# Put-off second steps, ACT's own sum for v's mean, a product on GpSimd and re-ordered early loads in a two-layer hybrid decoder kernel

## The chip, the cores and the metric

The kernel runs on one core of a Trainium2 chip. The metric is the device time of a run in microseconds (us), the median of three runs. TensorE is written PE (its weight loads PEld), VectorE DVE, ScalarE ACT, GpSimd POOL, and SyncE, which issues nearly all loads, SP. All weights come from HBM in each run (163 MB), all arithmetic is in 32 bits.

## What is computed

Two layers (DEPTH) on 256 tokens of 1,024 features, then a last normalization:

```python
def hybrid_layer(x, ...):
    h = rmsnorm(x, norm_mix)
    cb, cc, cu, q, k, v, g, ga, gb = split(h @ w_in)         # 1024 -> 9216
    y_conv = (cb * conv3(cc * cu)) @ w_conv_out               # causal, 3 taps per channel
    y_ret = retention(rotary(q), rotary(k), v), per head: (o - mean(o)) * rsqrt(var(o)), * silu(g), @ w_ret_out
    merged = sigmoid(ga) * y_conv + sigmoid(gb) * y_ret
    x = x + merged @ w_o
    h2 = rmsnorm(x, norm_mlp)
    return x + square(relu(h2 @ w_up)) @ w_down               # 1024 -> 4096 -> 1024
```

The kernel takes the mean of o over a head's features out of v instead: v minus its own mean over the head (the function `value`).

## The kernel before, in words

**Blocks.** The weights are cut into 152 blocks of 1 MB, in the order of use; activations lie with features on partitions and the 256 tokens along the free dimension. Each block is one step of the program, a *window* (`window`, `proj`). A layer has 76: v (4 blocks), then `IN_ORDER`: g, g, (cc, cu, cb) twice, q, q, k, k, (cc, cu, cb) twice, g, g, ga x4, gb x4; then the products with w_conv_out (4), w_ret_out (4), w_o (4), w_up (16) and w_down (4 x 4 blocks into one sum).

**Two parts of every operand.** An fp32 value is written as a rounded fp32r part (hi) and the rest (lo): `split` makes hi with a copy on ACT (L103) and lo with a subtraction on DVE (L104). A block's product is 16 matmuls of 512 columns (hi weight by both parts of the activation) and 16 of 256 (lo weight by the activation's hi), all on PE at L165. So every block of weights costs two ACT casts and two DVE subtractions of 128x1024 (`split_block`, two halves), in tiles of the program's names `raw` (2 buffers) and `parts` (3 buffers). Block i+2 is split in window i; the load of block i+3 is issued at that window's end, on SP.

**Order.** Nothing schedules this: the engines run their instructions in the order in which the code emits them. `at(n, fn, ...)` puts a step in the list of the window n further on; in one window the list's steps of phase 0 come first, in the order in which they were put in, then the first half of block i+2, the steps of phase 1, the second half, and then the block's matmuls. What the list emits for one engine therefore stands ahead of that engine's share of the splitting of block i+2.

**Evictions.** The product of block i is in one of three PSUM buffers (`ps_main`); in window i+1 it is taken out by `collect`: an ACT copy of one half (L235) and a DVE sum of both (L236) to SBUF. What follows it is the function named after the operand: `gate`, `conv_u`, `conv_in`, `conv_b`, `conv_out`, `rotate`, `merge_gate`, `up_out`, `add_to_x`. `up_out` goes on in the same window with a ReLU (L710) and a square (L711) on ACT; the product with the norm's factor is on POOL one window later (L712) and the split of u another window later. `value` is v's: DVE sums 4 x 256 columns (L462), scales the sum (L463), and ACT and DVE make hi (L467), lo (L468) and v1 (L472) out of PSUM in turns. `conv_out` multiplies by cb on DVE (L518) and splits in the same window. `weigh_scores` weighs on DVE (L534, L535) and splits at once. `head_roots` to `head_out` make 1/std of a head: square root on ACT (L572), reciprocal on DVE (L577) one window later, a Newton step the next, the product (L587) and its split in the two windows after. `add_to_x` adds to x (L683) and splits the sum for the next norm (L271 on ACT, L276 on DVE) at once, then squares it between the two halves of the block's split.

**The tail of each sum.** `head_sums` makes PE sum the squares of a head (tile `var_ps`) behind a window's block; it needs the split of `osq` of that window. `norm_total` does the same for a norm.

Of the kernel before, what the change touches and what calls it, by code (L numbers as in the profile page):

```python
# [11 lines left out]
F32 = mybir.dt.float32  # L12
# [3 lines left out]
AF = mybir.ActivationFunctionType  # L16
# [36 lines left out]
def trunk_kernel(ctx, tc, px, pos, w, cst, mask, out):  # L53
# [260 lines left out]
    k0 = 0  # L314
    for n in (1, 3, 4):
        c = slice(n_par + k0 * T if k0 else 0, n_par + (k0 + n) * T)
        nc.scalar.dma_start(out=px_sb[:, c], in_=px[:, c])
        k0 += n
    for c in (slice(0, 4), slice(4, 8), slice(8, 16)):
        nc.sync.dma_start(out=raws[0][:, c, :], in_=w0[:, c, :])  # L320
    nc.sync.dma_start(out=raws[1].rearrange("p a b -> p (a b)"), in_=w[1])

# [75 lines left out]
    for layer in range(DEPTH):  # L398
# [59 lines left out]
        def value(i, ps):  # L458

            mu = small.tile([P, 2, 2], F32, tag="mu", name="mu")  # L460
            vs = ps.rearrange("p j (h f) -> p j h f", f=T)
            nc.vector.tensor_reduce(out=mu, in_=vs, axis=mybir.AxisListType.X, op=ALU.add)  # L462
            nc.vector.tensor_scalar(out=mu, in0=mu, scalar1=-1.0 / T, scalar2=None, op0=ALU.mult)  # L463
            for n in range(2):
                h = 2 * i + n
                hi, lo = v0_parts[:, 0, h, :], v0_parts[:, 1, h, :]
                nc.scalar.activation(hi, vs[:, 0, n, :], AF.Identity, bias=mu[:, 0, n:n + 1])  # L467
                nc.vector.scalar_tensor_tensor(  # L468
                    out=lo, in0=vs[:, 0, n, :], scalar=mu[:, 0, n:n + 1], in1=hi.bitcast(F32),
                    op0=ALU.add, op1=ALU.subtract,  # L470
                )
                nc.scalar.activation(v1[:, h, :], vs[:, 1, n, :], AF.Identity, bias=mu[:, 1, n:n + 1])  # L472
# [40 lines left out]
        def conv_b(p, ps_b):  # L513
            y = collect(ps_b)
            at(1, conv_out, p, y)

        def conv_out(p, y):
            nc.vector.tensor_tensor(out=y, in0=y, in1=conv[p], op=ALU.mult)  # L518
            split(y, *yc.pair(p))
# [12 lines left out]
        def weigh_scores(h, ps):  # L532
            t = t2("sc0")[:, 0, :]
            nc.vector.tensor_tensor(out=t, in0=ps[:, :T], in1=mask_sb[:, h, :], op=ALU.mult)  # L534
            nc.vector.tensor_tensor(out=sc1[:, h, :], in0=ps[:, T:], in1=mask_sb[:, h, :P], op=ALU.mult)  # L535
            split(t, sc0_parts[:, 0, h, :], sc0_parts[:, 1, h, :])
# [29 lines left out]
        def head_roots(i, st):  # L566
# [12 lines left out]
            for n in range(2):  # L579
                at(3 + n, head_out, 2 * i + n, rs[:, n, :])  # L580

        def head_out(h, rs):

            if h % 2 == 0:
                yr.tiles.append(s8.tile([P, KT // 2, 2, T], F32R, tag="s8", name=f"yr{h // 2}"))
            y = sg[:, 2 * h:2 * h + 2, :]
            nc.vector.tensor_tensor(out=y, in0=y, in1=both(rs), op=ALU.mult)  # L587
            split(y, *yr.pair(h))
# [89 lines left out]
        def add_to_x(p, ps, scale, norm, parts=True):  # L678

            for j in range(2):  # L680
                xk = x[:, 2 * p + j, :]
                for half in (1, 0):
                    nc.vector.scalar_tensor_tensor(  # L683
                        out=xk, in0=ps[:, j, half, :], scalar=scale, in1=xk, op0=ALU.mult, op1=ALU.add
                    )
            if parts:
                for j in range(2):
                    norm.split_hi(2 * p + j)
                for j in range(2):
                    norm.split_lo(2 * p + j)  # L690
            at(0, norm.square, p, ph=1)
            if p == NPAIR - 1:
                at(0, norm.fold, ph=1)
                at(1, norm.split_sum)

# [184 lines left out]
```

## Time and profile before

| | before |
|---|---|
| three runs, us | 946.89, 949.07, 946.75 |
| median, us | 946.89 |
| the profiled execution, us | 945.4 |
| its span, first to last instruction, us | 943.6 |
| PE / PEld busy in it, us (share) | 898.1 (95%) / 772.1 (82%) |
| DVE busy | 709.9 (75%) |
| ACT busy | 510.5 (54%) |
| POOL busy | 230.0 (24%) |
| chain that ended last, by engine | DVE 44%, PE 25%, ACT 18%, issue 8%, POOL 3%, DMA 3% |
| mean TensorE clock granted | 0.984 of full |

A matmul's end is modelled in the profile, so "busy" of PE is an upper bound of its useful time; the chain of work that ended last goes through DVE more than through PE. A row of a timeline reads: start in the span, time, engine, line, operation, output<-inputs, shapes, count; in brackets the engine's idle time before it and what ended it.

### The profile page before, as it was taken

The numbers are of one execution on the slowest core, as the hardware profiler recorded it, in microseconds if no ns is written. First come the engines' busy times: TensorE is split into PE (matmuls) and PEld (weight loads), VectorE is DVE, ScalarE is ACT, GpSimd is POOL, SyncE is SP. The second block draws the span as 40 slices with busy tenths as digits, with TensorE's granted clock in tenths as the row PEclk, the third lists the DMA queues.
The fourth block names the chain that finished last, engine by engine and source line by source line (L and its number), as shares of the span: only waits on it lengthen the run. The fifth ranks groups of instructions, "written<-read, shape, count | busy, mean of one in ns | idle before, by whom it ended". The sixth has DMA issues, their size and how long they took to land.

```text
span 943.6 us, 12548 instructions
## 1 busy us (share of the span) xinstructions
PE 898.1 (95%) x5026; PEld 772.1 (82%) x5026; DVE 709.9 (75%) x800; ACT 510.5 (54%) x709; POOL 230.0 (24%) x160
## 2 busy tenths in 40 slices
PE   9898999989999999999998999998999999999996
PEld 5687788877887887788887888887878887778896
DVE  4688998989987666665567899998888856666651
ACT  5555445745554666744444544555555566675450
POOL 0635542422112221200110545242202222220110
PEclk9899999999999999999999999999999999999998
DMA  7534444434654444475553554454355444446531
GB/s 266 179 140 165 172 177 151 166 134 161 236 181 139 174 177 161 161 259 186 202 191 126 187 179 150 163 179 159 129 207 181 173 156 164 172 179 223 210 148 44
DMA packets 23674, 163.00 MB, mean 173 GB/s; under 512 B 2752, under 2 KB 3008, under 8 KB 4288
## 3 DMA queue, kind: packets, MB, share of 16 engines
q1 hardware_dynamic: 22896, 160.57, 47.9%
q10 hardware_dynamic: 720, 1.63, 0.5%
q8 instruction: 39, 0.64, 0.3%
q14 instruction: 19, 0.16, 0.0%
HBM read 161.14 MB, written 1.05 MB: 172 GB/s over the span
## 4 chain that ended last, share of the span: by engine, by line
DVE 44%; PE 25%; ACT 18%; issue 8%; POOL 3%; DMA 3%; SPq 0%; DVEq 0%; ACTq 0%; POOLq 0%
DVE parts L104 26%; PE ps L165 24%; ACT parts L103 8%; DVE sum L236 4%; DMA raw<-w 3%; ACT sum L710 2%; ACT u L711 2%; DVE up L104 2%; DVE rot L450 1%; DVE px_sb L683 1%; POOL ta L490 1%; ACT sum L235 1%; DVE acc L504 1%; ACT L572 1%; DVE sum L518 1%
## 5 line engine op out<-in xcount | busy, mean ns | idle before, releaser
L104 DVE TENSOR_TENSOR parts<-raw,parts 128x1024 fp32r<-128x1024 f32 x305 | 436.2, 1465 | 155.4 <-ACT parts L103 154.1
L103 ACT CAST parts<-raw 128x1024 fp32r<-128x1024 f32 x305 | 306.2, 1047 | 89.4 <-DMA raw<-w 60.2
L165 PE MATMUL ps<-mix,parts 128*128 128x512 f32 (+1 forms) x1792 | 329.0, 345 | 15.0 <-DVE parts L104 7.4
L165 PEld LDWEIGHTS ps<-mix,parts 128*128 128x128 f32 x1792 | 280.5, 192 | 59.1 <-DVE parts L104 9.9
L165 PE MATMUL ps<-mlp,parts 128*128 128x512 f32 (+1 forms) x1024 | 185.9, 341 | 7.9 <-DVE parts L104 4.8
L165 PEld LDWEIGHTS ps<-mlp,parts 128*128 128x128 f32 x1024 | 157.6, 190 | 35.5 <-DVE parts L104 10.4
L165 PE MATMUL ps<-up,parts 128*128 128x512 f32 (+1 forms) x1088 | 181.3, 328 | 1.4 <-DVE parts L104 1.4
L165 PEld LDWEIGHTS ps<-up,parts 128*128 128x128 f32 x1088 | 160.3, 189 | 21.8 <-DVE parts L104 3.3
L712 POOL TENSOR_TENSOR u<-u,rr2m 128x512 f32<-128x512 f32 x32 | 41.8, 1308 | 153.3 <-ACT u L711 136.2
L236 DVE TENSOR_TENSOR sum<-ps,sum 128x512 f32<-128x512 f32 x78 | 53.1, 680 | 2.4 <-ACT sum L235 1.8
L710 ACT ACTIVATE sum<-sum 128x512 f32<-128x512 f32 x32 | 20.2, 632 | 63.5 <-DVE sum L236 63.5
L165 PE MATMUL ps<-yc,parts 128*128 128x512 f32 (+1 forms) x256 | 48.8, 349 | 4.9 <-DVE parts L104 4.8
L165 PEld LDWEIGHTS ps<-yc,parts 128*128 128x128 f32 x256 | 40.4, 194 | 13.0 <-DVE parts L104 7.1
L235 ACT COPY sum<-ps 128x512 f32<-128x512 f32 x78 | 45.1, 578 | 6.8 <-PE ps L165 6.8
L285 POOL TENSOR_TENSOR mix_sum<-mix_sum,sq 128x512 f32<-128x512 f32 x8 | 12.8, 1600 | 145.4 <-ACT sq L283 145.3
L165 PE MATMUL ps<-mg,parts 128*128 128x512 f32 (+1 forms) x256 | 45.4, 338 | 0.1
L165 PE MATMUL ps<-yr,parts 128*128 128x512 f32 (+1 forms) x256 | 45.1, 338 | 0.0
L165 PEld LDWEIGHTS ps<-mg,parts 128*128 128x128 f32 x256 | 39.2, 188 | 6.0 <-DVE mg L670 0.4
L165 PEld LDWEIGHTS ps<-yr,parts 128*128 128x128 f32 x256 | 39.2, 188 | 5.6
L165 PE MATMUL ps<-parts,mix 128*128 128x512 f32 x180 | 41.5, 390 | 1.0 <-ACT parts L103 1.0
L165 PEld LDWEIGHTS ps<-parts,mix 128*128 128x128 f32 x180 | 33.6, 188 | 8.8 <-ACT parts L103 1.8
L631 POOL TENSOR_TENSOR sum<-sum,rr 128x512 f32<-128x512 f32 x8 | 12.2, 1527 | 76.7 <-DVE sum L236 76.7
(174 smaller groups left out, 644.1 us busy)
## 6 DMA issues: line engine op xcount, KB each, us to landing
raw<-w SPq DMA_DIRECT2D x151, 1024.0 KB, 4.8
raw<-w SPq DMA_DIRECT2D x2, 256.0 KB, 4.7
raw<-w SPq DMA_DIRECT2D x1, 512.0 KB, 7.4
px_sb<-px ACTq DMA_DIRECT2D x1, 512.0 KB, 7.9
mask_sb<-mask SPq DMA_DIRECT2D x1, 512.0 KB, 5.7
out<-o SPq DMA_DIRECT2D x2, 256.0 KB, 2.3
out<-o ACTq DMA_DIRECT2D x2, 256.0 KB, 2.4
px_sb<-px ACTq DMA_DIRECT2D x1, 384.0 KB, 5.5
```

The lines of the kernel that those rows point to most:

```text
L103: nc.scalar.copy(hi, src)
L104: nc.vector.tensor_tensor(out=lo, in0=src, in1=hi.bitcast(F32), op=ALU.subtract)
L165: nc.tensor.matmul(o, lhsT=a, rhs=b, start=start, stop=stop, skip_group_check=True)
L235: nc.scalar.copy(t, ps[:, :, 1, :])
L236: nc.vector.tensor_tensor(out=t, in0=ps[:, :, 0, :], in1=t, op=ALU.add)
L285: nc.gpsimd.tensor_tensor(out=self.sum, in0=self.sum, in1=sq, op=ALU.add)
L450: nc.vector.tensor_tensor(out=w_[64:128], in0=t[0:64], in1=both(sinr[0:64, :]), op=ALU.mult)
L490: nc.gpsimd.tensor_tensor(out=d, in0=d, in1=both(rr), op=ALU.mult)
L631: nc.gpsimd.tensor_tensor(out=z, in0=z, in1=both(rr2), op=ALU.mult)
L710: nc.scalar.activation(rl, rl, AF.Relu)
L711: nc.scalar.activation(u, rl, AF.Square)
L712: at(1, lambda: nc.gpsimd.tensor_tensor(out=u, in0=u, in1=both(rr2), op=ALU.mult))
```

## The change

Seven edits of order and engine; no matmul, no weight and no size changes.

1. **Early loads.** x and the parameters (`px`) came in three pieces on ACT's queue (1, 3 and 4 feature tiles). Now tiles 0 and 1 come on ACT's queue, tiles 2 and 3 on SP's behind the first block's three pieces, then block 1, then tiles 4 to 7.
2. **`value`.** ACT copies v out of PSUM in four pieces of 256 columns, each with its sum as a second output (`accum_out`); DVE's sum over PSUM goes. One window later `less_mean` makes hi on ACT, v1 now on DVE, and lo on DVE, from SBUF.
3. **conv's last product.** POOL multiplies by cb right after the eviction, behind its own product of `conv_in`; the split comes one window later, as before.
4. **`weigh_scores`.** The split comes one window later.
5. **`head_out`.** The product stands one window earlier (in the window of the Newton step for the first head), its split where it was.
6. **`add_to_x`.** For pairs 0 to 2 the split and the square come one window later, in phase 0; for the last pair the split stays.
7. **`up_out`.** ReLU, square and POOL's product come one window later, together; the split of u stays in its window.

```diff
+    def load_x(q, k, n):
+        c = slice(n_par + k * T if k else 0, n_par + (k + n) * T)
+        q.dma_start(out=px_sb[:, c], in_=px[:, c])
+
+    load_x(nc.scalar, 0, 1)
+    load_x(nc.scalar, 1, 1)
     for c in (slice(0, 4), slice(4, 8), slice(8, 16)):
         nc.sync.dma_start(out=raws[0][:, c, :], in_=w0[:, c, :])
+    load_x(nc.sync, 2, 2)
     nc.sync.dma_start(out=raws[1].rearrange("p a b -> p (a b)"), in_=w[1])
+    load_x(nc.sync, 4, 4)
...
-            nc.vector.tensor_reduce(out=mu, in_=vs, axis=mybir.AxisListType.X, op=ALU.add)
+            t = [t2("vt") for _ in range(2)]
+            for j in range(2):
+                for n in range(2):
+                    nc.scalar.activation(
+                        t[j][:, n, :], ps[:, j, n * T:(n + 1) * T], AF.Copy, accum_out=mu[:, j, n:n + 1]
+                    )
             nc.vector.tensor_scalar(out=mu, in0=mu, scalar1=-1.0 / T, scalar2=None, op0=ALU.mult)
+            at(1, less_mean, i, t, mu)
...
         def conv_b(p, ps_b):
-            y = collect(ps_b)
-            at(1, conv_out, p, y)
-
-        def conv_out(p, y):
-            nc.vector.tensor_tensor(out=y, in0=y, in1=conv[p], op=ALU.mult)
-            split(y, *yc.pair(p))
+            y, acc = collect(ps_b), conv[p]
+            nc.gpsimd.tensor_tensor(out=acc, in0=y, in1=acc, op=ALU.mult)
+            at(1, split, acc, *yc.pair(p))
...
-            split(t, sc0_parts[:, 0, h, :], sc0_parts[:, 1, h, :])
+            at(1, split, t, sc0_parts[:, 0, h, :], sc0_parts[:, 1, h, :])
...
-                at(3 + n, head_out, 2 * i + n, rs[:, n, :])
+                at(2 + n, head_out, 2 * i + n, rs[:, n, :])
...
             nc.vector.tensor_tensor(out=y, in0=y, in1=both(rs), op=ALU.mult)
-            split(y, *yr.pair(h))
+            at(1, split, y, *yr.pair(h))
...
+            end = p == NPAIR - 1
             if parts:
-                for j in range(2):
-                    norm.split_hi(2 * p + j)
-                for j in range(2):
-                    norm.split_lo(2 * p + j)
-            at(0, norm.square, p, ph=1)
-            if p == NPAIR - 1:
+                at(0 if end else 1, x_parts_of, p, norm)
+            at(0 if end or not parts else 1, norm.square, p, ph=1 if end or not parts else 0)
+            if end:
...
         def up_out(p, ps, rr2=rr2):
-            rl, u = collect(ps), t2("u")
+            at(1, up_square, p, collect(ps))
+
+        def up_square(p, rl, rr2=rr2):
+            u = t2("u")
             nc.scalar.activation(rl, rl, AF.Relu)
             nc.scalar.activation(u, rl, AF.Square)
-            at(1, lambda: nc.gpsimd.tensor_tensor(out=u, in0=u, in1=both(rr2), op=ALU.mult))
-            at(2, up_parts, p, u)
+            nc.gpsimd.tensor_tensor(out=u, in0=u, in1=both(rr2), op=ALU.mult)
+            at(1, up_parts, p, u)
```

ACT in two windows of the w_up stage, before (`sum` is the evicted product, `u` its squared ReLU, `parts` the next weights' hi):

```order
L235 COPY sum<-ps 128x512
L710 ACTIVATE sum<-sum 128x512
L711 ACTIVATE u<-sum 128x512
L103 CAST parts<-raw 128x1024 x2
L103 CAST up_2948<-u 128x2x256
L235 COPY sum<-ps 128x512
L710 ACTIVATE sum<-sum 128x512
L711 ACTIVATE u<-sum 128x512
L103 CAST parts<-raw 128x1024 x2
```

and in the changed kernel:

```order
L728 ACTIVATE sum<-sum 128x512
L729 ACTIVATE u<-sum 128x512
L235 COPY sum<-ps 128x512
L103 CAST parts<-raw 128x1024 x2
L103 CAST up_2956<-u 128x2x256
L728 ACTIVATE sum<-sum 128x512
L729 ACTIVATE u<-sum 128x512
L235 COPY sum<-ps 128x512
L103 CAST parts<-raw 128x1024 x2
```

ReLU and square, which read DVE's sum, stood between the copy out of PSUM and the casts of the weights; now they stand ahead of the copy and read the sum of the window before.

DVE around v in the first layer (window 4 and 5), before (`mu` the mean, `mix_sl` the norm's sum, `sg` the first g):

```order
L104 TENSOR_TENSOR parts<-raw,parts 128x1024 x6
L462 TENSOR_REDUCE mu<-ps 128x4
L463 TENSOR_SCALAR mu<-mu 128x4
L468 SCALAR_TENSOR_TENSOR v_parts<-ps,mu,v_parts 128x256 x2
L104 TENSOR_TENSOR parts<-raw,parts 128x1024 x2
L104 TENSOR_TENSOR mix_sl<-mix_sum,mix_sh 128x256
L462 TENSOR_REDUCE mu<-ps 128x4
```

and in the changed kernel:

```order
L104 TENSOR_TENSOR parts<-raw,parts 128x1024 x6
L471 TENSOR_SCALAR mu<-mu 128x4
L104 TENSOR_TENSOR parts<-raw,parts 128x1024 x2
L104 TENSOR_TENSOR mix_sl<-mix_sum,mix_sh 128x256
L471 TENSOR_SCALAR mu<-mu 128x4
L478 TENSOR_SCALAR v_144<-vt,mu 128x256 x2
L483 SCALAR_TENSOR_TENSOR v_parts<-vt,mu,v_parts 128x256 x2
```

No instruction of DVE reads v's PSUM any more, and only the scaling of mu stands ahead of the weights' split in window 4.

DVE in the window of the second `var_ps` sums, before (`rs_a`, `rm` the Newton step, `osq` what PE sums, `ta` the next eviction):

```order
L104 TENSOR_TENSOR parts<-raw,parts 128x1024 x2
L241 TENSOR_TENSOR rs_a<-rm 128x512
L242 SCALAR_TENSOR_TENSOR rs_a<-rs_a,rm 128x512
L243 SCALAR_TENSOR_TENSOR rm<-rs_a,rm 128x512
L104 TENSOR_TENSOR osq<-osq 128x256
L236 TENSOR_TENSOR ta<-ps,ta 128x512
```

and in the changed kernel:

```order
L104 TENSOR_TENSOR parts<-raw,parts 128x1024 x2
L241 TENSOR_TENSOR rs_a<-rm 128x512
L242 SCALAR_TENSOR_TENSOR rs_a<-rs_a,rm 128x512
L243 SCALAR_TENSOR_TENSOR rm<-rs_a,rm 128x512
L598 TENSOR_TENSOR sg<-sg,rm 128x512
L104 TENSOR_TENSOR osq<-osq 128x256
L236 TENSOR_TENSOR ta<-ps,ta 128x512
```

The product of `head_out` now stands ahead of the split that PE's sums need.

## Rows read from the trace of the kernel before

**Rows 1.** Waits of PE: what it waited for, us in total, times, longest

```profile
PE ps L165 <- DVE parts L104: 18.4, 37, 1.7
PE ps L165 <- ACT v L472: 7.0, 3, 4.6
PE var_ps L165 <- DVE osq L104: 6.1, 2, 3.1
PE ps L165 <- DVE mlp L276: 3.1, 2, 1.9
```

**Rows 2.** Busy time by stretch; PEclk is the granted share of the clock

```profile
39.10:45.90 6.80, 6.17 (x19) 5.30 (x20) 4.96 (x6) 2.95 (x5) 6.29 (x7) 0.50 0.23 67
687.70:691.00 3.30, 3.30 (x12) 2.82 (x11) 2.31 (x4) 2.32 (x4) 0.00 (x0) 0.50 0.52 174
```

**Rows 3.** Timeline of PE in both w_up stages, first and last of a row

```profile
342.60 5.83 PE L165 MATMUL ps<-mlp,parts 128*128 128x256 f32 x32 [0.32 <-DVE parts L104]
...
348.73 5.83 PE L165 MATMUL ps<-mlp,parts 128*128 128x256 f32 x32 [0.30 <-DVE parts L104]
...
854.33 7.90 PE L165 MATMUL ps<-up,parts 128*128 128x256 f32 x44 [0.23 <-DVE parts L104]
```

**Rows 4.** Timeline of PE: a block that waits for nothing, and the next instruction

```profile
586.72 5.80 PE L165 MATMUL ps<-mix,parts 128*128 128x512 f32 x32
592.35 0.52 PE L165 MATMUL sc_ps<-q_parts,k_parts 128*128 128x256 f32 x3
```

**Rows 5.** Timeline of ACT, POOL and DVE in one window of w_up

```profile
357.19 0.63 ACT L710 ACTIVATE sum<-sum 128x512 f32<-128x512 f32 x1 [1.96 <-DVE sum L236]
...
358.39 1.99 ACT L103 CAST parts<-raw 128x1024 fp32r<-128x1024 f32 x2
358.56 1.30 POOL L712 TENSOR_TENSOR u<-u,rr2m 128x512 f32<-128x512 f32 x1 [4.83 <-ACT u L711]
359.46 2.63 DVE L104 TENSOR_TENSOR parts<-raw,parts 128x1024 fp32r<-128x1024 f32 x2 [2.30 <-ACT parts L103]
```

**Rows 6.** Busy time of PE, PEld, DVE, ACT, POOL by stretch, first layer

```profile
128.00:198.00 70.00, 66.38 (x396) 58.20 (x394) 65.01 (x76) 41.81 (x61) 22.75 (x15) 1.00 0.48 169
```

**Rows 7.** Timeline around v's eviction in the first layer

```profile
34.00 0.63 ACT L283 ACTIVATE sq<-px_sb 128x512 f32<-128x512 f32 x1
...
35.27 1.22 DVE L462 TENSOR_REDUCE mu<-ps 128x4 f32<-128x1024 f32 x1
...
39.20 0.47 ACT L472 ACTIVATE v<-ps,mu 128x256 f32<-128x256 f32 x1 [0.55 <-DVE v_parts L468]
...
39.73 1.65 PE L165 MATMUL ps<-mix,parts 128*128 128x512 f32 x4 [4.58 <-ACT v L472]
```

**Rows 8.** Timeline of DVE and POOL: conv's product, and splits beside POOL and alone

```profile
97.92 0.68 DVE L518 TENSOR_TENSOR sum<-sum,acc 128x512 f32<-128x512 f32 x1
...
99.29 0.69 DVE L104 TENSOR_TENSOR yc<-sum,yc 128x512 fp32r<-128x512 f32 x1 [0.69 <-ACT yc L103]
...
177.18 3.45 DVE L104 TENSOR_TENSOR parts<-raw,parts 128x1024 fp32r<-128x1024 f32 x2
...
177.33 2.21 POOL L490 TENSOR_TENSOR ta<-ta,rr 128x512 f32<-128x512 f32 x1 [2.70 <-DVE ta L236]
...
239.88 2.36 DVE L104 TENSOR_TENSOR parts<-raw,parts 128x1024 fp32r<-128x1024 f32 x2
```

**Rows 9.** Timeline of DVE: the scaling beside the square root of the second sums

```profile
206.04 0.69 DVE L573 TENSOR_SCALAR rm<-var_ps 128x512 f32<-128x512 f32 x1 [1.84 <-ACT rm L572]
```

**Rows 10.** Waits of PE: from 128 to 240 us, then from 560 to 700

```profile
PE ps L165 <- DVE parts L104: 3.1, 4, 1.7
PE var_ps L165 <- DVE osq L104: 3.1, 1, 3.1
...
PE ps L165 <- DVE parts L104: 3.7, 5, 1.7
PE var_ps L165 <- DVE osq L104: 3.0, 1, 3.0
```

**Rows 11.** Timeline of ACT at the start

```profile
9.07 1.04 ACT L103 CAST parts<-raw 128x1024 fp32r<-128x1024 f32 x1 [1.81 <-DMA raw<-w]
```

More of the change, by code (lines that the diff above doesn't have):

```diff
@@ L313, in trunk_kernel @@
     w0 = w[0].rearrange("p (a b) -> p a b", b=P)
[L314 to L318, printed above, removed]
+    def load_x(q, k, n):
[3 more added lines that the diff above has]
+    load_x(nc.scalar, 1, 1)
     for c in (slice(0, 4), slice(4, 8), slice(8, 16)):
         nc.sync.dma_start(out=raws[0][:, c, :], in_=w0[:, c, :])
+    load_x(nc.sync, 2, 2)
     nc.sync.dma_start(out=raws[1].rearrange("p a b -> p (a b)"), in_=w[1])
+    load_x(nc.sync, 4, 4)
     nc.scalar.activation(eps2, eps, AF.Square)
@@ L460, in value, with less_mean @@
             mu = small.tile([P, 2, 2], F32, tag="mu", name="mu")
-            vs = ps.rearrange("p j (h f) -> p j h f", f=T)
-            nc.vector.tensor_reduce(out=mu, in_=vs, axis=mybir.AxisListType.X, op=ALU.add)
+            t = [t2("vt") for _ in range(2)]
[4 more added lines that the diff above has]
+                    )
             nc.vector.tensor_scalar(out=mu, in0=mu, scalar1=-1.0 / T, scalar2=None, op0=ALU.mult)
+            at(1, less_mean, i, t, mu)
+        def less_mean(i, t, mu):
             for n in range(2):
                 h = 2 * i + n
-                hi, lo = v0_parts[:, 0, h, :], v0_parts[:, 1, h, :]
-                nc.scalar.activation(hi, vs[:, 0, n, :], AF.Identity, bias=mu[:, 0, n:n + 1])
+                nc.scalar.activation(v0_parts[:, 0, h, :], t[0][:, n, :], AF.Identity, bias=mu[:, 0, n:n + 1])
+                nc.vector.tensor_scalar(
+                    out=v1[:, h, :], in0=t[1][:, n, :], scalar1=mu[:, 1, n:n + 1], scalar2=None, op0=ALU.add
+                )
+            for n in range(2):
+                h = 2 * i + n
                 nc.vector.scalar_tensor_tensor(
-                    out=lo, in0=vs[:, 0, n, :], scalar=mu[:, 0, n:n + 1], in1=hi.bitcast(F32),
-                    op0=ALU.add, op1=ALU.subtract,
+                    out=v0_parts[:, 1, h, :], in0=t[0][:, n, :], scalar=mu[:, 0, n:n + 1],
+                    in1=v0_parts[:, 0, h, :].bitcast(F32), op0=ALU.add, op1=ALU.subtract,
                 )
-                nc.scalar.activation(v1[:, h, :], vs[:, 1, n, :], AF.Identity, bias=mu[:, 1, n:n + 1])
         def gate(p, ps, n):
@@ L685, in add_to_x, with x_parts_of @@
                     )
+            end = p == NPAIR - 1
             if parts:
-                for j in range(2):
-                    norm.split_hi(2 * p + j)
-                for j in range(2):
-                    norm.split_lo(2 * p + j)
-            at(0, norm.square, p, ph=1)
-            if p == NPAIR - 1:
+                at(0 if end else 1, x_parts_of, p, norm)
+            at(0 if end or not parts else 1, norm.square, p, ph=1 if end or not parts else 0)
+            if end:
                 at(0, norm.fold, ph=1)
                 at(1, norm.split_sum)
+        def x_parts_of(p, norm):
+            for j in range(2):
+                norm.split_hi(2 * p + j)
+            for j in range(2):
+                norm.split_lo(2 * p + j)
         norm = Norm(gains(layer, G_MLP), f"mlp{layer}")
```

## The prediction, made before the result was known

> **What bounds the kernel now.** I read the page first: PE is "busy" 95% of the span, yet the chain of work that ended last is 44% DVE and 25% PE, so PE is fed late in places. The waits of PE say where [rows 1]: 18.4 us on DVE's lo parts of the weights, 7.0 on v's eviction, 6.1 on the splits of the variance sums, 3.1 on the splits of x before w_up; 34.6 us together. The second price is the clock. The stretches with a granted clock of 0.50, PE's lower level (1.2 GHz), are 39.1 to 45.9 and five more of 3.4 us at 80, 200, 295, 653 and 688 (a seventh is the end) [rows 2]. Each follows a pause of PE of 1.7 to 4.6 us. PE is busy in them, at half speed, so they cost half their length: 3.4 and five times 1.7. Waits and clock together are some 46 us; that is what the change can give back at most, but for a few tenths of refilling per wait.
>
> A block that waits for nothing takes PE 5.63 us (592.35 less 586.72) [rows 4]. In the w_up stages it takes 6.13 (348.73 less 342.60), over 10 windows in the first layer and 13 in the second [rows 3]. All engines go round once there [rows 5]: DVE's sum, ACT's ReLU and square, the first cast, DVE's two subtractions, DVE's split of u, the next sum. ACT stood idle 1.96 us for the sum, DVE 2.30 us for the casts. Elsewhere DVE itself is the bound: from 128 to 198 it is busy 65.0 of 70 us [rows 6].
>
> **The change part by part.**
>
> *w_up (edit 7).* ACT's copy is now followed by the casts, and ReLU and square read a sum that has lain ready for a window, so the circle is cut. ACT has four operations of 128x512 at 0.63 and casts of 1.99, 4.5 us a window, DVE two at 0.68 [rows 8] and 2.63, 4.0 us; both lie below 5.63, so PE is what is late next. The blocks' 23 waits go: 23 x (6.13 - 5.63) = 11.5 us. Bounds: 6 us (the idle PE time of the rows alone, about 0.27 each) and 11.5. I take the upper, since it is read start to start. POOL's product moves in front of ACT's cast of u; its 1.30 us [rows 5] has the copy and both casts (2.6 us) for cover.
>
> *Splits of x (edit 6).* Pairs 0 to 2 no longer make ACT and DVE wait for each other inside a window, so DVE comes to the last pair before PE has ended its block. PE's two waits (3.1 us) [rows 1] and the slow clock at 295 (1.7) go: 4.8. The work that goes into the last window (0.96 us of DVE) is done while PE still runs the block before. Bounds: 2 to 4.8, if DVE stays late by half.
>
> *v (edit 2), second layer.* ACT is idle when v is done, so its four copies take PSUM empty within a block. Of PE's 7.0 us on v [rows 1] 4.58 stand in the first layer [rows 7]; the other 2.4 go. No row shows a copy with a sum as second output. The nearest is the 0.47 us of 256 columns out of PSUM [rows 7]; from above I bound it with twice that. Even then four of them (3.8 us) lie inside one block of 5.63. So the second layer doesn't depend on it.
>
> *v, first layer, to the end of k.* ACT's square ends at 34.63; four copies of 0.47 end at 36.5, at 38.4 by the upper bound, instead of 39.67 [rows 7]. I take 36.5: PE then waits 1.4 instead of 4.58 us, which is below the pauses that a low clock followed, and 39.1 to 45.9 runs at full speed: 3.2 + 3.4 = 6.6. Not all stays, because DVE then sets the pace up to the k blocks. DVE itself gains two sums of 1.22 [rows 7], some 3 us of taking turns with ACT (ACT's 0.47 six times), and two of conv's products (below); it loses four v1 of about 0.4 (estimate: a little under ACT's 0.47 for the same width): 2.4 + 3 + 1.7 - 1.6 = 5.5. The smaller number counts: 5.5, with bounds 2 (copies at twice the price, POOL's angle tables late) and 6.6.
>
> *Conv's product, score splits, head products (edits 3 to 5), rest of the mixing stages.* DVE loses 0.68 and its wait of 0.69 for ACT per product [rows 8]. The product costs POOL 1.3 to 2.2 us, and beside such an operation a pair of DVE subtractions takes 3.45 instead of 2.36 us [rows 8]: up to 1.1 back; I take half, 0.55, since POOL's product also falls on idle time of DVE. Net 0.8 each. The rule against this edit is in the Trainium skill, GPSIMD Engine Reference, sections Engine selection and Key points: elementwise work with two inputs belongs on VectorE, GpSimd is about half as fast and shares VectorE's interfaces to SBUF. The rows agree (2.21 against 0.68 us, and 1.1 us on the neighbour); taken at its full price, the sum below would be 8 x 0.55 = 4.4 us smaller.
> Four score splits a layer no longer hold DVE for ACT (about 1.9 us a layer); the four products of heads lose their 0.69 each, and 1.84 goes at the square root [rows 9], because ACT needn't wait for DVE first. Against it, `head_out`'s 0.68 now stands ahead of `osq`. Per layer that is 1.6 + 1.9 + 2.8 + 1.8 - 0.7 = 7.4 us of DVE time. PE waited 3.1 + 3.7 us on DVE's parts there, and 6.1 at the second variance sums of the layers [rows 10]. With 7 us less on DVE the 6.8 go; of the variance waits I keep 1.5 of 6.1, because of the product put in front. With these pauses go the low clocks at 200, 653 and 688: 3 x 1.7. Together 6.8 + 4.6 + 5.1 = 16.5; bounds 5 (full POOL price, low clocks stay) and 18.
>
> *Early loads (edit 1).* PE waits 1.0 us at 9.2 for the first block's second half, which ACT got at 9.07 [rows 11]. Loads that this half doesn't need now start behind it. 1.0 us; bounds 0 and 1.5. The Trainium skill (DMA: Bandwidth & Descriptors, Issuing engines are not separate DMA queues) says that queues of different engines share the same 16 DMA engines; by that alone a change of queue would give nothing, and the sum would be 1.0 smaller. No row here separates queue from order.
>
> **The sum.** 11.5 + 4.8 + 2.4 + 5.5 + 16.5 + 1.0 = 41.7 us. The profiled execution took 945.4 (its span 943.6), so 903.7; the median lay 1.5 above it: 905.
>
> **The rivals.**
> *DVE keeps the mixing stages.* POOL's products and the denser order lengthen DVE's subtractions by their full price, low clocks come with the next pause, and half of the 22.0 us of both mixing terms is given back: 905 + 11 = 916. For it: DVE is busy 93% there [rows 6], with nothing to hide behind. Against it: what goes is mostly waiting.
> *Only the waits between ACT and DVE go.* The mixing stages gain nothing: 11.5 + 4.8 + 2.4 = 18.7, so 928. For it: the first layer's head also hangs on POOL's tables. Against it: v's eviction and the clock behind it.
> *It doesn't do what it says.* The circle in w_up closes another way (copy, casts and subtractions still follow PE's end too late) and 11.5 goes back: 905 + 11.5 = 916.5.
> *Slower than before.* ACT's first instruction of a w_up window is now the cast of u, which needs POOL's product, and behind it in ACT's order stand ReLU, square, the copy that frees PSUM and the casts. POOL's 1.30 [rows 5] and three ACT operations of 0.63 make a ring of 3.2 us. It binds from a POOL product of 3.7 us on. To eat the whole gain, 32 windows would have to lose 1.3 us below 5.63, that is a product of some 5 us and 947 or more; a little above, 950. The longest that rows show is 2.21 [rows 8].
>
> **How the numbers follow.** The forecast (895 to 911) gets 0.58, the DVE rival 0.20, the uncut circle 0.06, waits alone 0.10, slower 0.03, no change 0.03. The likeliest time is 905. The range goes from 895 (all bounds at their best, 45 us, and some refilling) to 922, which leaves out the last three and a little of the first. About 0.3% is what a measurement of this kernel can tell from no change. Faster by more: 0.94; within: 0.03; slower by more: 0.03.
>
> **What would show it.** In the changed profile: blocks of w_up 5.6 us apart and no wait of PE on DVE's parts there; no wait on v in the second layer and one below 2 us in the first, with the clock at 1.00 around 40; at most one low stretch per layer's mixing stage; PE's four kinds of wait [rows 1] near 10 us in all instead of 34.6; conv's products on POOL at 1.3 to 2.2 us. Wrong if DVE's subtractions grow well above 3.45 us a pair, if copies with a sum take more than 0.9 us, or if PE waits on u's split or on PSUM.

## The result and the profile after

| | before | changed |
|---|---|---|
| median of four runs, us | 947.13 | 907.38 |
| all runs, us | 946.75 to 949.07 | 905.73, 905.77, 908.98, 909.50 |
| ratio, 95% interval | | 0.9578 [0.9548, 0.9607] |
| the profiled execution / its span, us | 945.4 / 943.6 | 909.5 / 907.7 |

The forecast was 905 (895 to 922). From the page of the changed kernel, the busy times and the chain of work that ended last:

```profile
PE 885.3 (98%) x5026; PEld 764.6 (84%) x5026; DVE 709.2 (78%) x796; ACT 512.9 (57%) x733; POOL 258.0 (28%) x168
...
PE 64%; DVE 23%; issue 4%; POOL 3%; DMA 3%; ACT 2%; SPq 0%; DVEq 0%; ACTq 0%; POOLq 0%
```

The chain now runs through PE for 64% of the span; before it was 25%, with DVE at 44%. The waits of PE, to be read against [rows 1]:

```profile
PE ps L165 <- DVE parts L104: 7.5, 8, 1.7
PE var_ps L165 <- DVE osq L104: 2.4, 2, 1.6
...
PE ps L165 <- ACT parts L103: 1.2, 1, 1.2
PE ps L165 <- DVE sum L236: 1.0, 2, 0.7
PE ps L165 <- DVE sg L236: 0.8, 1, 0.8
PE ps L165 <- ACT vt L468: 0.5, 1, 0.5
```

On DVE's parts PE waits 8 times instead of 37, on v 0.5 us instead of 7.0, on the splits of x not at all. All eight waits on parts lie ahead of 125 us. The prediction's sign for the four kinds of wait together was "near 10 us"; they are 10.4. Up to 903.7 us, where the last products are done, the clock is at 1.00 throughout in this execution. The other three have mean granted clocks of 0.993, 0.995 and 0.993 against 0.998 here, which is some 9 to 13 us at half clock where this one has 4 at its end (an estimate from the means). So a clock without low stretches is shown for the execution with the trace alone.

**Where the 36 us of the span come from.** Both kernels have the same 5,026 matmuls in the same order, so I took the time from start to start of all neighbours and compared it with 230.2 ns (512 columns) and 116.5 ns (256 columns), the pace of an undisturbed stretch of the kernel before. What a gap has above that is put down as clock if the granted clock is 0.50 there, else as a wait if it is over 40 ns, and else as pace (the first matmuls, which take longer in full fp32, and the waits at the start and the end are among the waits of every kernel). In us:

| kernel | span | waits | low clock | pace |
|---|---|---|---|---|
| before | 943.6 | 58.3 | 10.8 | 5.4 |
| changed | 907.7 | 26.1 | 0 | 12.6 |

Waits and clock fell by 43.0 us, a little more than the 41.7 forecast. The last column took 7.2 back, and no step of the prediction had it: at a granted clock of 1.00 PE itself has two paces. The rows are the four blocks of w_ret_out (128 matmuls, no wait) and the start of the next stage, of before and then of the changed kernel:

```profile
242.99 22.35 PE L165 MATMUL ps<-yr,parts 128*128 128x512 f32 x128
265.18 21.02 PE L165 MATMUL ps<-mg,parts 128*128 128x512 f32 x118
```

```profile
232.14 22.77 PE L165 MATMUL ps<-yr,parts 128*128 128x512 f32 x128
254.75 22.77 PE L165 MATMUL ps<-mg,parts 128*128 128x512 f32 x128
```

22.19 us against 22.61, that is 5.55 against 5.65 a block, or 346.7 against 353.3 ns for a pair of 512 and 256 columns. Single pairs vary (at the slow pace they take about 350, 350 and 360 ns in turn), but averaged over nine pairs nearly every stretch of both traces has one of these two values, for up to hundreds of pairs on end. They go from one to the other where PE has waited or other matmuls stood between; one change, at 574 us in the kernel before, has no such break. In the profile of before 4 of 10 pairs run at the slow one, in that of the changed kernel 9 of 10.

### The profile page after: what moved, and what is told of

The parts are those of the page before. It is cut to its first block, busy times and chain, and to the rows that moved or that the text cites. A ratio compares the mean times of both kernels' runs of the same rounds, so it can differ in the third digit from the quotient of the medians.

```text
span 907.7 us, 12561 instructions
## 1 busy us (share of the span) xinstructions
PE 885.3 (98%) x5026; PEld 764.6 (84%) x5026; DVE 709.2 (78%) x796; ACT 512.9 (57%) x733; POOL 258.0 (28%) x168
## 4 chain that ended last, share of the span: by engine, by line
PE 64%; DVE 23%; issue 4%; POOL 3%; DMA 3%; ACT 2%; SPq 0%; DVEq 0%; ACTq 0%; POOLq 0%
PE ps L165 64%; DVE parts L104 14%; DMA raw<-w 3%; DVE sum L236 2%; DVE rot L454 1%; ACT parts L103 1%; DVE acc L518 1%; DVE yc L104 1%; POOL ta L504 0%; POOL red L369 0%; DVE sg L565 0%; DVE sg L498 0%; DVE acc L521 0%; POOL ang L384 0%; DVE sg L236 0%
## 5 line engine op out<-in xcount | busy, mean ns | idle before, releaser
L165 PE MATMUL ps<-mix,parts 128*128 128x512 f32 (+1 forms) x1792 | 322.9, 340 | 11.0 <-DVE parts L104 7.5
L165 PEld LDWEIGHTS ps<-mix,parts 128*128 128x128 f32 x1792 | 274.5, 188 | 54.8 <-DVE parts L104 10.0
L165 PE MATMUL ps<-mlp,parts 128*128 128x512 f32 (+1 forms) x1024 | 181.6, 340 | 0.0
L730 POOL TENSOR_TENSOR u<-u,rr2m 128x512 f32<-128x512 f32 x32 | 46.1, 1441 | 131.3 <-ACT u L729 118.3
L285 POOL TENSOR_TENSOR mix_sum<-mix_sum,sq 128x512 f32<-128x512 f32 x8 | 12.6, 1574 | 155.7 <-ACT sq L283 155.6
L165 PE MATMUL ps<-yc,parts 128*128 128x512 f32 (+1 forms) x256 | 45.6, 340 | 0.0
L694 DVE SCALAR_TENSOR_TENSOR px_sb<-ps,px_sb 128x256 f32<-128x256 f32 x60 | 24.0, 421 | 15.6 <-PE ps L165 14.6
L642 POOL TENSOR_TENSOR sum<-sum,rr 128x512 f32<-128x512 f32 x8 | 15.8, 1979 | 59.2 <-DVE sum L236 59.2
```

What stands on the lines that cost most here:

```text
L165: nc.tensor.matmul(o, lhsT=a, rhs=b, start=start, stop=stop, skip_group_check=True)
L285: nc.gpsimd.tensor_tensor(out=self.sum, in0=self.sum, in1=sq, op=ALU.add)
L642: nc.gpsimd.tensor_tensor(out=z, in0=z, in1=both(rr2), op=ALU.mult)
L694: nc.vector.scalar_tensor_tensor(out=xk, in0=ps[:, j, half, :], scalar=scale, in1=xk, op0=ALU.mult, op1=ALU.add)
```

## The experiments

In "changed with edit n undone" everything else stays. The table has the median of all runs of each kernel and, from its one profiled execution, the same columns as above:

| kernel | median (range), us | waits | clock | pace |
|---|---|---|---|---|
| changed | 907.4 (905.7 to 909.5) | 26.1 | 0 | 12.6 |
| e1, w_up undone | 916.7 (916.6 to 920.7) | 35.0 | 0 | 10.8 |
| e2, v undone | 913.3 (908.9 to 914.0) | 32.4 | 1.5 | 4.3 |
| e3, conv's product on DVE | 910.7 (906.7 to 911.9) | 27.6 | 6.1 | 2.1 |
| e4, scores and heads undone | 919.7 (917.2 to 921.3) | 38.9 | 1.5 | 6.0 |
| e5, splits of x undone | 907.7 (906.5 to 910.8) | 30.5 | 1.5 | 6.2 |
| e6, angles early | 904.6 (904.1 to 905.5) | 21.8 | 1.5 | 10.6 |
| e8, squares first | 905.2 (904.4 to 905.6) | 25.0 | 3.5 | 5.0 |
| e9, order in pairs | 904.1 (903.9 to 904.3) | 28.9 | 1.5 | 3.1 |
| f1, e9 + conv's product on DVE | 908.1 (907.7 to 908.4) | 29.1 | 4.6 | 3.2 |
| f2, before in pairs | 944.8 (943.7 to 945.7) | 61.2 | 8.9 | 3.9 |
| f3, e9 + first layer's head | 896.7 (896.6 to 898.8) | 21.4 | 1.4 | 3.2 |
| g1, f3 + squares first | 897.5 (897.2 to 897.7) | 23.5 | 0 | 3.3 |

In the old order of matmuls the pace of one execution differs from that of the next by up to 10 us, and the changed kernel's own four runs lie 3.8 us apart. A difference of two medians there is good to a few us only; the waits of the traces, and the runs in the order of e9, say more.

**e1: w_up undone.**

```diff
-            at(1, up_square, p, collect(ps))
+            rl, u = collect(ps), t2("u")
+            nc.scalar.activation(rl, rl, AF.Relu)
+            nc.scalar.activation(u, rl, AF.Square)
+            at(1, lambda: nc.gpsimd.tensor_tensor(out=u, in0=u, in1=both(rr2), op=ALU.mult))
+            at(2, up_parts, p, u)
```

> The changed kernel with edit 7 (w_up's ReLU, square and product one window later) undone, all else kept. If the circle of sum, ReLU, square, casts and subtractions set the pace of w_up and edit 7 alone cut it, 23 blocks stand 6.13 us apart again instead of 5.65 (what the changed kernel's trace shows), PE waits 0.2 to 0.3 us per block on DVE's parts there, and the time is 907.4 + 11 = 918 (range 916 to 921). If the faster rest of the kernel (casts one window earlier, x split later) would have fed w_up by itself, the time stays at 906 to 910. If only the idle time counts and not the refilling, it is 907.4 + 6 = 913.

916.7 us, 9.3 more. PE in the w_up stage of e1:

```profile
346.81 5.83 PE L165 MATMUL ps<-mlp,parts 128*128 128x256 f32 x32 [0.31 <-DVE parts L104]
352.94 5.82 PE L165 MATMUL ps<-mlp,parts 128*128 128x256 f32 x32 [0.30 <-DVE parts L104]
```

The blocks stand 6.13 us apart again with the old wait [rows 3]. The changed kernel has none in the same stretch:

```profile
344.73 20.54 PE L165 MATMUL ps<-mlp,parts 128*128 128x512 f32 x115
```

Only 18 blocks are late (9 a layer, 23 before), and 18 x 0.49 is 8.8. The circle is the cause, and undoing edit 7 alone brings it back; five of the 23 late blocks stay away without it.

**e2: v undone.** `value` as before, with DVE's sum and the turns of ACT and DVE on PSUM.

```diff
-                    nc.scalar.activation(
-                        t[j][:, n, :], ps[:, j, n * T:(n + 1) * T], AF.Copy, accum_out=mu[:, j, n:n + 1]
-                    )
...
+            nc.vector.tensor_reduce(out=mu, in_=vs, axis=mybir.AxisListType.X, op=ALU.add)
```

> The changed kernel with edit 2 (v out of PSUM by four ACT copies with sums) undone. The forecast's sizes: PE waits 4.58 us and 2.4 us on v again, a low clock of 6.8 us follows the first, so 907.4 + 2.4 + 6.6 = 916. What the trace of the changed kernel suggests instead: the wait is late at v or, a few windows later, at POOL's angle tables, which end at 49.1 us in it and at 48.6 in the kernel before; then only about 2.4 us of the first layer's 6.6 come back beside 3.0 of the second layer's: 912.8 (range 911 to 914). If edit 2 does nothing in the first layer: 910.

913.3 us, which the second case names (911 to 914), with waits on v as before (the profiled execution is the fastest of the five, 908.9, with 8.3 us less of pace than the changed kernel's):

```profile
PE ps L165 <- ACT v L476: 7.9, 4, 4.3
...
PE ps L165 <- DVE parts L104: 5.7, 6, 1.4
```

**e3 and f1: conv's product.** Both put it back on DVE.

```diff
-            nc.gpsimd.tensor_tensor(out=acc, in0=y, in1=acc, op=ALU.mult)
-            at(1, split, acc, *yc.pair(p))
+            at(1, conv_out, p, y)
+
+        def conv_out(p, y):
+            nc.vector.tensor_tensor(out=y, in0=y, in1=conv[p], op=ALU.mult)
+            split(y, *yc.pair(p))
```

> The changed kernel with edit 3 (conv's last product on POOL) undone: eight products of 0.68 us on DVE again, with its wait for ACT behind each. As the forecast sized it (net 0.8 us of DVE per product, on the path): 907.4 + 8 x 0.8 = 914, with PE's waits on DVE's parts in the mixing stages grown by some 6 us from 7.5. If POOL's product costs DVE its full price (1.1 us on the subtractions beside it): 909 to 910. If POOL's 2.15 us (the eight in the changed kernel's trace) disturb DVE by more than they spare, it is faster than 907: about 904. A product that only falls into waits that stay: 907.

910.7 us: between the cases. Its waits and clock are 7.6 us above the changed kernel's, but some 3.4 of it is a low clock of 6.8 us at 61.9, behind a pause that the changed kernel has too, there without one; and the pace is 10.5 us lower. So I repeated it in the order of e9 (below), which has one pace:

> The changed kernel with the order of matmuls of the run before (512, 512, 256, 256), which held one pace of PE, and conv's last product on DVE again. Settles what edit 3 is worth without the two paces: in the run with the product on DVE and the old order, PE's waits and low clocks in the profile were 7.5 us more than in the changed kernel, but the time only 3.3 more. If the waits are the worth and the pace hid the rest: 904.1 + 7 = 911. If the time is the worth: 907.4. If the product's place is of no account: 904.

908.1 against 904.1: 4.0 us, and the ranges don't touch. The second case (907.4) is nearest: 0.5 us per product. The price on DVE's subtractions shows in its groups from 128 to 198 us, where two of the products lie: e9, then f1, in the same order of matmuls (x, busy us, mean ns, idle before):

```profile
L104 DVE TENSOR_TENSOR parts<-raw,parts 128x1024 fp32r<-128x1024 f32 x23 | 40.8, 1813 | 0.8 <-ACT parts L103 0.7
```

```profile
L104 DVE TENSOR_TENSOR parts<-raw,parts 128x1024 fp32r<-128x1024 f32 x23 | 38.6, 1716 | 0.8 <-ACT parts L103 0.7
```

The same 23 subtractions take 2.2 us more beside two products on POOL (2.15 us each): 1.1 each. Record by record, one subtraction beside each of these two products takes 2.31 us instead of 1.21. What the 4.0 us consist of is less plain: from e9 to f1 the table's waits grow by 0.2 us and the low clock by 3.1 (three stretches of 3.4 us instead of one).

**e4: scores and heads undone.**

```diff
-            at(1, split, t, sc0_parts[:, 0, h, :], sc0_parts[:, 1, h, :])
+            split(t, sc0_parts[:, 0, h, :], sc0_parts[:, 1, h, :])
...
-                at(2 + n, head_out, 2 * i + n, rs[:, n, :])
+                at(3 + n, head_out, 2 * i + n, rs[:, n, :])
...
-            at(1, split, y, *yr.pair(h))
+            split(y, *yr.pair(h))
```

> The changed kernel with edits 4 and 5 (splits of weighed scores one window later, head products one window earlier) undone. By the forecast's shares (5.8 of the 7.4 us of DVE time a layer) these two carry most of the 16.5 us of the mixing stages: 907.4 + 13 = 920, with the waits at the second variance sums near 3 us each and the slow clock behind them back. If either of the three edits alone would be enough to keep DVE ahead: 908 to 910. If the head product in front of the split of the squares costs as much as the rest brings: 907.

919.7 us, as the first case has it, and with the waits that it names (2.7 us each; a low clock follows the first of them and not the second):

```profile
PE ps L165 <- DVE parts L104: 12.9, 14, 1.7
PE var_ps L165 <- DVE osq L104: 5.4, 2, 2.7
```

**e5: splits of x undone.**

```diff
-                at(0 if end else 1, x_parts_of, p, norm)
-            at(0 if end or not parts else 1, norm.square, p, ph=1 if end or not parts else 0)
+                x_parts_of(p, norm)
+            at(0, norm.square, p, ph=1)
```

> The changed kernel with edit 6 (splits of pairs 0 to 2 of x one window later) undone. As the forecast sized it, PE waits 1.9 and 1.2 us on the splits of x before w_up again and a low clock follows the longer one: 907.4 + 4.8 = 912. If the earlier windows of w_o are now early enough by themselves (DVE no longer comes late out of the mixing stages), the waits stay away: 906 to 908. If only the waits come back and no clock: 910.5.

907.7 us, no difference that these runs can tell: the time of the second case, and yet the waits of the third are back:

```profile
PE ps L165 <- DVE mlp L276: 2.9, 2, 1.5
...
PE ps L165 <- DVE mg L681: 1.0, 1, 1.0
```

3.9 us of waits returned, and the pace is 6.4 us lower in the same profile, because PE ran more of its pairs at the fast one. The time alone would have said that the edit is worth nothing. It was not repeated in the order of e9, so what edit 6 is worth in time stays open.

**e6: angle tables early.** Not an undoing: it asks what is late in the first layer's head.

```diff
-            at(4, reduce_angles)
-            at(7, sines)
-            at(8, rotation_tables)
+            at(2, reduce_angles)
+            at(5, sines)
+            at(6, rotation_tables)
```

> The changed kernel with POOL's angle tables two windows earlier (the reduction in window 2, the sines in 5, the tables in 6). Tests why the first layer's head gave back 2.4 us and not 5.5. If the reduction, which ends at 49.1 us in the changed kernel and holds DVE for 4.22 us and then ACT for 8.9, is what is late next there, PE's waits between 50 and 76 us (6.3 us: 0.77, 0.58, 1.16, 1.72, 0.73 and 1.34) go for the most part: 907.4 - 4.5 = 903 (range 901 to 904). If DVE's own work is the bound there, the waits only move to the parts of the weights: 906 to 908. If the reduction now delays the norm's sum of squares, which POOL adds up in the same windows: 909 or more.

In the changed kernel (ACT, DVE and PE, from 48 to 63 us):

```profile
49.15 0.42 ACT L391 ACTIVATE sh<-ang 128x256 f32<-128x256 f32 x1 [2.79 <-POOL ang L384]
58.47 0.42 ACT L392 ACTIVATE turns<-turns 128x256 f32<-128x256 f32 x1 [8.90 <-DVE turns L390]
...
49.15 0.43 DVE L241 TENSOR_TENSOR rs_a<-rr 128x256 f32<-128x256 f32 x1 [4.22 <-POOL ang L384]
...
60.35 0.49 PE L165 MATMUL ps<-mix,parts 128*128 128x512 f32 x1 [1.16 <-ACT parts L103]
62.57 7.68 PE L165 MATMUL ps<-mix,parts 128*128 128x256 f32 x43 [1.72 <-DVE parts L104]
```

DVE's Newton step waits for POOL's reduction, ACT waits for it too and then for DVE, and behind ACT's sine stand the casts that PE needs. The Newton step reads nothing of the angles. By the code its tile `rs_a` comes out of the same six buffers (`tmp1`) as the reduction's tiles, so it likely waits for a buffer and not for a value; no run tests that. In e6 all waits of PE from 50 to 76 us are gone; a new one came (ACT, then PE):

```profile
41.15 0.41 ACT L103 CAST mix_sh<-mix_sum 128x256 fp32r<-128x256 f32 x1 [4.12 <-POOL mix_sum L289]
...
45.10 17.16 PE L165 MATMUL ps<-mix,parts 128*128 128x512 f32 x88 [2.64 <-ACT vt L468]
```

The reduction now stands ahead of the norm's sums on POOL, ACT waits for them, and v's second pair of copies is behind that. 904.6 us: that the tables' place makes those waits is confirmed, the cure is half. (e6 moves the reduction, the sines and the tables together, so their shares are not parted.)

**e8: squares first.** The Newton step and `head_out` move to phase 1, behind the first half of the weights' split.

```diff
-            at(2, lambda: newton(rs, t2("rs_a", "rs", 1), rm[:, 1, h, :]))
+            at(2, lambda: newton(rs, t2("rs_a", "rs", 1), rm[:, 1, h, :]), ph=1)
...
-                at(2 + n, head_out, 2 * i + n, rs[:, n, :])
+                at(2 + n, head_out, 2 * i + n, rs[:, n, :], ph=1)
```

> The changed kernel with the Newton step and the head product of a window put between the two halves of the weights' split, so that the split of the squares that PE sums stands ahead of them on DVE. PE waits 1.6 and 0.8 us at the second variance sums in the changed kernel. If the 2.8 us of DVE in front of that split are the cause, both waits go and the weights' parts still come in time: 907.4 - 2.4 = 905. If DVE has no slack there, the wait comes back one block later on DVE's parts: 907 to 908.

905.2 us is the number of the first case, and still that case is wrong: the waits on `osq` are gone, but 2.5 us on DVE's parts came at 209, 219, 644 and 654 us, and the lower time is pace (5.0 instead of 12.6). The profile says that DVE has no slack there, and g1 settles it.

**e9 and f2: the order of a block's matmuls.**

```diff
                 for j in range(2):
-                    first, end = ...
                     mm(ps[:, j], blk[:, 0, 2 * k + j, :], a, first, False)
+                for j in range(2):
                     mm(ps[:, j, 1], blk[:, 1, 2 * k + j, :], a[:, 0], False, end)
```

> The changed kernel with the matmuls of a block in the order 512, 512, 256, 256 columns instead of 512, 256, 512, 256. Tests what was not foreseen: at a granted clock of 1.00 PE runs a pair of 512 and 256 columns in 346.7 or in 353.3 ns, for hundreds of pairs on end, and changes between the two only where it has stopped; the changed kernel's profile has nine of ten pairs at 353.3, the one before four of ten. If the alternation of the two lengths makes the slow pace, the new order holds one pace at 346 to 347 ns per pair and the time is 907.4 - 12 = 895. If the pace does not hang on the order: 905 to 909, with the two paces seen again. If two short matmuls in a row leave the next weight load uncovered: above 346.7 everywhere, by up to 20 ns a pair, that is 907 to 940.

```profile
232.06 22.46 PE L165 MATMUL ps<-yr,parts 128*128 128x512 f32 x128
254.35 22.61 PE L165 MATMUL ps<-mg,parts 128*128 128x512 f32 x128
```

One pace only: 22.29 us for four blocks, 5.57 each, in all stages without waits. That is 0.08 below the slow pace and 0.02 above the fast. 9.5 us of pace are gone, but the time gains 3.3: PE comes earlier to stages where DVE is the bound, and waits there (the two on `osq` are 2.05 us each, not 1.6 and 0.8). Waits and low clock took 4.3 back; the rest is that the changed kernel's profiled execution lies 2.1 above its median. The expected 895 left that out. The four runs now lie within 0.4 us instead of 3.8.

> The kernel before with its matmuls in the order 512, 512, 256, 256, nothing else. In its profile 5.4 us are the slow pace of PE. If the seven edits are worth the same with either order, and PE's pace took some of their gain back in the changed kernel, this gains less than the changed kernel did (3.3 us), since its blocks wait for DVE anyway: 944 to 946, that is 40 us or more above the 904.1 of the changed kernel in that order. If the pace counts in full here: 941.7. If it gains nothing: 947.

944.8 us, 2.2 below the kernel before (ratio 0.9975 [0.9966, 0.9985]), as the first case has it. From f2 to e9 the seven edits are worth 40.7 us, in the old order 39.8.

**f3 and g1: a better kernel.** f3 is e9 with the angle reduction cut in two around the norm's sums, and without a second split of block 5 that the code does in window 3.

```diff
-        for half in range(2):
-            at(3, split_half, 5, half, ph=2)
...
-        for c in (c1, c2, c3, c4):
+        for c in (c1, c2):
...
-            at(4, reduce_angles)
-            at(7, sines)
-            at(8, rotation_tables)
+            at(2, reduce_angles, 0)
+            at(4, reduce_angles, 1)
+            at(6, sines, ph=2)
+            at(7, rotation_tables)
```

> The changed kernel in the order 512, 512, 256, 256, with two edits in the first layer's head: POOL's angle reduction cut in two halves (window 2 and window 4, so that the norm's sums stand between them; the sines in window 6 behind the split, the tables in window 7), and without the second split of block 5, which the code does twice. With the whole reduction in front of the sums the waits between 50 and 76 us had gone, but ACT waited 4.1 us for the late sums and PE 2.6 us and a low clock for v behind them. If this order avoids both, PE's waits of that stretch (6.5 us) go: 904.1 - 6 = 898. If the sums of the norm are late again: 903 to 905. If DVE's waits move to the windows behind: 901.

896.7 us, ratio 0.9475 [0.9461, 0.9489] to the kernel before, 1.2% below the changed one. What the second of the two edits gave of it was not measured by itself. No wait of PE is left between 28 and 67 us:

```profile
28.34 11.30 PE L165 MATMUL ps<-mix,parts 128*128 128x512 f32 x64
39.47 0.28 PE L165 MATMUL mix_st<-mix_sh,ones 128*128 128x256 f32 x1
39.59 0.28 PE L165 MATMUL mix_st<-mix_sl,ones 128*128 128x256 f32 x1
39.71 22.45 PE L165 MATMUL ps<-mix,parts 128*128 128x512 f32 x128
```

> All that helped, together: the order 512, 512, 256, 256, the first layer's head as in the run before, and the Newton step and head product between the two halves of the weights' split. With the faster pace of PE the waits at the second variance sums had grown from 2.4 to 4.4 us with a low clock (1.7) behind one of them. If they go and waits of some 2.5 us on DVE's parts two and four blocks later take their place, as in the single run of that edit: 896.7 - 3.6 = 893 (range 892 to 894.5). If DVE has no slack at all: 896 to 897. If the later waits bring low clocks: 898.

897.5 us, no gain: the second case. Two waits on `osq` (4.4 us) and a low clock went, and these came:

```profile
PE ps L165 <- DVE parts L104: 6.5, 10, 1.3
PE ps L165 <- DVE tb L237: 1.7, 2, 0.9
PE ps L165 <- DVE mg L687: 1.4, 2, 0.8
```

f3 has 4.4 on parts there. In e8 and here, DVE had no slack, and the wait came back where its work was put.

## Why the prediction was right, point by point

The k-th matmul of both traces is the same one, so the difference of their starts, read at the borders of the stages, gives each term in us, pace included:

| term | forecast | by starts | undone, in time |
|---|---|---|---|
| w_up | 11.5 | 10.9 | 9.3 (e1) |
| splits of x, MLP start | 4.8 | 4.7 | 0.3 (e5) |
| v, second layer | 2.4 | 3.0 | |
| v, first layer, to the end of k | 5.5 | 2.4 | both v: 6.0 (e2) |
| rest of the mixing stages | 16.5 | 16.7 | 12.3 (e4), 3.3 to 4.0 (e3, f1) |
| early loads | 1.0 | 1.0 | |

They add up to 38.7; stretches without waits, where the changed kernel ran at the slow pace, gave 3.1 back. No run undoes edit 1, so whether the order of the loads or their queue gave its 1.0 stays open.

**w_up.** Right in mechanism and size. The unstalled block that the term was measured against (5.63 [rows 4]) ran at the fast pace, 5.55, and lost 0.08 at its first matmul, behind other matmuls (315 ns instead of 230). At 5.55 throughout the term would have been 13, at the slow 5.65 it is 11; the agreement with 10.9 hangs on the pace that the changed kernel happened to have.

**Splits of x.** The waits went as forecast. e5 brings 3.9 us of waits back and no low clock behind them (the one in its profile is at 62 us): of the 1.7 for the clock in the term nothing is shown by undoing. The low stretch at 295 us is in the trace of before, behind a pause of 1.89 us, and not in the changed kernel's; the pauses in e5 are 1.46 and 1.44.

**v.** The price with no row was below the bounds (0.47 and twice that): a copy with its sum is two instructions on ACT, and the next copy starts 0.36 us later:

```profile
33.03 0.37 ACT L468 ACTIVATE vt<-ps 128x256 f32<-128x256 f32 x1
33.30 0.19 ACT L468 ACTIVATION_READ_ACCUMULATOR vt<-ps 128x1 f32 x1
33.39 0.38 ACT L468 ACTIVATE vt<-ps 128x256 f32<-128x256 f32 x1
```

PE waits 0.5 us there instead of 1.4 as forecast, and the low clock is gone. That 1.4 "is below the pauses that a low clock followed" was a misreading: the low stretch at 80 us in the kernel before follows pauses of 0.56 and 1.34 us.

```profile
77.12 0.47 PE L165 MATMUL ps<-mix,parts 128*128 128x512 f32 x1 [0.56 <-DVE sum L236]
78.92 7.42 PE L165 MATMUL ps<-mix,parts 128*128 128x256 f32 x32 [1.34 <-DVE parts L104]
```

By 52 us this was worth 7.1 us; 5.3 of it were lost by 65 us, and at the end of the k blocks 4.7 were still gone. **This is the step that failed:** "Not all stays, because DVE then sets the pace up to the k blocks" summed DVE's own time, and left POOL's angle tables to the lower bound (2). They were what is late next: the reduction ends at 49.1 us in the changed kernel and at 48.6 before. It begins 1.5 us earlier in the changed kernel, but its first two operations take 3.7 us from start to start instead of 1.5. DVE and POOL in the changed kernel, then POOL before:

```profile
35.55 2.67 DVE L104 TENSOR_TENSOR parts<-raw,parts 128x1024 fp32r<-128x1024 f32 x2 [0.53 <-ACT parts L103]
...
35.76 1.39 POOL L374 CAST ang<-pos_i 128x256 f32<-128x256 int32 x1
37.26 2.09 POOL L369 TENSOR_SCALAR ang<-ang,cst_sb 128x256 f32<-128x256 f32 x1
...
48.38 0.73 POOL L384 TENSOR_TENSOR ang<-ang,red 128x256 f32<-128x256 f32 x1
```

```profile
37.22 0.39 POOL L370 CAST ang<-pos_i 128x256 f32<-128x256 int32 x1
37.72 0.92 POOL L365 TENSOR_SCALAR ang<-ang,cst_sb 128x256 f32<-128x256 f32 x1
...
47.85 0.74 POOL L380 TENSOR_TENSOR ang<-ang,red 128x256 f32<-128x256 f32 x1
```

In e2, with v undone, the same operations run as fast as before and the reduction ends at 46.9. So part of the lateness comes with edit 2: DVE, which in the kernel before mostly waited for ACT while these two ran, now subtracts beside POOL (35.55 to 38.2 us). That the one slows the other there is likely and not tested. e6 shows by moving the tables that they make the waits; f3 agrees, with a second edit beside it.

**Mixing stages.** The sum is right, its shares were not tested by rows alone. PE's waits on parts behind 128 us (6.8) went entirely, the three low clocks (5.1) too; of the 6.1 at the second variance sums [rows 10] 2.4 stay instead of 1.5, since the Newton step and the head's product stand ahead of the split. Conv's product was over-sized: 0.8 us each was forecast with half of POOL's price. The price is paid in full (1.1 us), and 0.5 each (f1) is what is left. That is more than the 0.3 that 0.68 + 0.69 - 1.1 gives. In the one trace of each, most of the difference is low clock behind longer pauses (the two on `osq` are 2.6 us in f1 and 2.05 in e9) and not DVE time one for one. The Trainium skill (GPSIMD Engine Reference, Engine selection and Key points) says that GpSimd shares its SBUF interfaces with VectorE and contends with VectorE instructions that have two SBUF inputs, and keeps elementwise work on VectorE. The 1.1 us agree with the first. The advice didn't hold here by the 4.0 us of f1; that the move also took away a wait of DVE for ACT is the likely reason, not tested by itself.

**The rivals.** "DVE keeps the mixing stages" (916) didn't come: from 128 to 198 us DVE is busy 67.1 of 70 us, even more than before [rows 6], and PE waits there for `osq` alone. e8, e9 and g1 show how near it was: each change that brings PE there earlier only moves the wait. "Only the waits between ACT and DVE go" (928) and the uncut circle (916.5) didn't come: the mixing stages gave 16.7 and w_up 10.9. "Slower" didn't come: POOL's product in w_up takes 1.44 us on average against the 3.7 from which its ring would bind.

**The end of the sum.** 945.4 - 41.7 + 1.5 gave 905; the profiled execution took 909.5, and the median of the four is 907.4. Waits and clock alone would have given more than forecast; the slow pace took it back. The profiled execution is 35.9 us faster, 5.8 short of the 41.7; about half of that is the lost part of v, the rest the pace. That the median is only 2.4 above 905 is in part luck, since two of the four runs came out 3.5 us faster than the one with the trace. Two of the four runs lie at 905.8 and two at 909; that the pace is what parts them is likely (in the order of e9 four runs lie within 0.4 us), but only one of the four has a trace.

## What to carry to other kernels

Where engines pass work around a circle inside one step, putting the second half of the circle one step later was worth the whole stall here, and the term could be read start to start from the trace. Where several stalls follow one another, the gain of removing the first is bounded by what is late next (here POOL's angle reduction, which began 1.5 us earlier and still ended 0.5 later): look for it by its end time in the trace, not by its share of busy time, and ask whether the change itself makes it slower. When undoing an edit changes the time by less than a stall that the trace shows, look whether the pace between the stalls moved too.

## What the runs showed of the hardware

- **Two paces of PE at full clock.** 512 and 256 columns in turn (fp32r, a new weight each) take 346.7 or 353.3 ns a pair; PE goes from one to the other nearly always where its stream is broken; 512, 512, 256, 256 takes 348.4 each time. Over 152 blocks the two would be 16 us apart. What chooses isn't known.
- **A low clock is not certain after a pause.** In e3 PE pauses 2.18 and 2.19 us at the second variance sums of the two layers:

```profile
193.59 0.50 PE L165 MATMUL var_ps<-osq,ones 128*128 128x512 f32 x1 [2.18 <-DVE osq L104]
...
629.79 0.51 PE L165 MATMUL var_ps<-osq,ones 128*128 128x512 f32 x1 [2.19 <-DVE osq L104]
```

The clock fell to 0.50 at 195 us, for 3.4 us, and not at all in the second layer. In all profiles here, seven of eleven single pauses of 2.0 to 2.7 us were followed by it, and all seven of 3 us and more. Shorter ones were at times too (1.73 us at 687.0 in the kernel before). Counting 1.7 us behind every such pause, as the forecast did, is the likely case and not a rule.

- **A product on POOL slows a subtraction on DVE.** Beside conv's product on POOL (128x512, 2.15 us) a subtraction of 128x1024 on DVE takes 2.31 us, without it 1.21 (e9 and f1 at 138 and 155 us).
